# Three elementwise steps put on GpSimd in a four-layer sequence model, and one of two products with ones left out

## The chip, the cores and the metric

The kernel runs on one core of one Trainium2 chip. The metric is the device time of one execution in microseconds (us), the median over several runs. The profile lists the core's engines: PE (TensorE products) and PEld (its weight loads), DVE (VectorE), ACT (ScalarE), POOL (GpSimd) and SP (which issues the DMAs here).

## What is computed

A sequence of 256 tokens of width 1024 passes two blocks of two layers each. The first block has, twice, a mixer (compressed, selected and sliding-window attention, a gated linear attention and a pooling branch) and a feed-forward part. The second block puts 16 meta tokens in front (272 rows) and has a layer of a gated linear recurrence (RG-LRU) beside attention over a sliding window with sinks, a layer of the Mamba-2 kind, and a feed-forward part behind each. Cut to what the change touches:

```python
# first block, sliding-window and selected attention
p = masked_softmax(s, m)                      # e / sum(e)
return jnp.einsum('bhgqk,bgkd->bhgqd', p, vb) # times a sigmoid gate per branch

# second block, first layer
y_a = gelu(gate) * rg_lru(xr, ...)            # the recurrence's gating
p_band = p_band / denom; p_meta = p_meta / denom

# second block, second layer (8 groups of 256 channels)
yg = yg * lax.rsqrt(jnp.mean(yg * yg, axis=-1, keepdims=True) + EPS)
```

## The kernel before

Activations lie with channels on the 128 partitions and tokens along the free dimension, so a tile is 128 x 256 or 128 x 272 (128 x 258 where the second-last layer needs only its last columns). Weights stream in as f32 chunks of up to 1 MB; each is split into a rounded part (`wh`, ScalarE, L257) and a rest (`wl`, VectorE, L258), and each weight tile of 128 x 128 is multiplied in three passes (`mm3`, L272 to L274). These passes are most of TensorE's 11685 instructions. The order of instructions on every engine is fixed when the program is built, by a scheduler that goes by the program's order and its own costs; `issue_after` puts a piece of work behind a given product, so that attention steps are dealt out between the projections' products. Every engine then works through its own list in order and waits where an operand or a buffer is not ready.

The places that the change touches:

- **`nsa.scores` (L815 to L841)**, first block, called for six (block of 128 tokens, head) pairs in each of its two layers. TensorE writes the scores of two key groups (L825), VectorE adds the mask and takes the maximum (L831), ScalarE takes the exponential and its sum (L833), VectorE the reciprocal and the branch gate (L835, L836), and then VectorE multiplies four pieces of `P` and `Pg` (128 x 128 or 128 x 256) by one number per row (L840). `transposes` (L777 is the shared transposing product) turns `P` and `Pg` for the product with the values.
- **`lru` (L1410 to L1420)**, second block's first layer, 8 tiles `k` of 128 x 272. VectorE takes two products (L1415, L1417), a scan along the tokens (L1419) and the gating `gt = l1 * gt` (L1420). `gt` is split much later (L282, L283) for the output projection.
- **`softmax` (L1467 to L1483)**, in the same layer: `attend` runs for two blocks of tokens and two halves of heads (tile `aP`, 8 pieces of 128 x 272 or 128 x 144) and `attend_meta` once (`aPq`, 2 pieces of 128 x 16). VectorE adds the bias and takes the row maximum while it empties the score banks (L1486), forms the exponent's offset (L1471 to L1473), ScalarE takes the exponentials (L1477), VectorE adds up and inverts (L1479, L1480) and multiplies the pieces (L1483). TensorE then transposes them (L1518 for the meta keys, L1528 for the others).
- **`ssd` (L1751 to L1833)**, second block's second layer, 8 groups `g`. ScalarE squares two tiles `sq` of 128 x 258 (L1828); TensorE adds them up over the partitions by two products with a matrix of ones that add up in one bank (L1832); ScalarE copies the sum out (L1833).

Of the kernel before, what the change touches and what calls it, by code (L numbers as in the profile page):

```python
# [10 lines left out]
OP = mybir.AluOpType  # L11
# [127 lines left out]
def view(ap, off, dims):  # L139

    return bass.AP(tensor=ap.tensor, offset=ap.offset + off, ap=[list(ap.ap[0])] + [list(d) for d in dims])
# [37 lines left out]
class Kern:  # L179
# [594 lines left out]
    def nsa(self, l, qT, kT, vsb, vc, sg, mh, ml):  # L774
        nc, p1, w1 = self.nc, self.p1, self.w1
        mm, V, A = nc.tensor.matmul, nc.vector, nc.scalar
# [38 lines left out]
        def scores(t, h):  # L815

            W = 128 * (t + 1)
            sp = [self.bank(x) for x in ("dd", "cb", "da", "ad", "ad", "ad")[3 * t + h]]
            P = (w1.tile([128, 512], F32, name="P", tag="P", bufs=3),
                 p1.tile([128, 512], F32, name="Pg", tag=f"tb{(h + t) % 2}"))  # L820
            m = w1.tile([128, 2, 2], F32, name="m2", tag="m2", bufs=4)
            sm = w1.tile([128, 2, 2], F32, name="s2", tag="s2", bufs=4)
            for b in range(2):

                self.pair(lambda g: mm(sp[g][:, b * W:b * W + W], lhsT=qT[gp[g], h, qs[t]], rhs=kT[gp[g], 1 + b, 0:W],  # L825
                                       start=True, stop=True))
            for b in range(2):
                for g in range(2):
                    c = slice(b * W, b * W + W)

                    V.tensor_tensor_reduce(P[g][:, c], sp[g][:, c], nm[:, 128 * t:128 * t + W], scale=-0.125,  # L831
                                           scalar=3.0e38, op0=OP.add, op1=OP.min, accum_out=m[:, b, g:g + 1])
                    A.activation(P[g][:, c], P[g][:, c], AF.Exp, scale=-1.0, bias=m[:, b, g:g + 1],  # L833
                                 accum_out=sm[:, b, g:g + 1])
            V.reciprocal(sm, sm)  # L835
            V.tensor_tensor(sm, sm, view(sg, t * 18 + 6 + 2 * h, [[6, 2], [1, 2]]), op=OP.mult)  # L836
            for g in range(2):
                for b in range(2):
                    c = slice(b * W, b * W + W)
                    V.tensor_scalar(P[g][:, c], P[g][:, c], sm[:, b, g:g + 1], None, op0=OP.mult)  # L840
            state[t, h] = P  # L841

        def transposes(t, h):
# [28 lines left out]
        def end(t):  # L872
            self.split(mh[:, 5:8, qs[t]], ml[:, 5:8, qs[t]], o[t][:, 0:384].rearrange("p (h q) -> p h q", h=3))
        compressed(0)
        scores(0, 0)
        yield
        scores(0, 1)
        yield
        compressed_T(0)
# [3 lines left out]
        for i, (t, h) in enumerate(heads):  # L883
            transposes(t, h)
            yield
            if h == 0:
                begin(t)
            outputs(t, h)
            if h == 2:
                end(t)  # L890
            if i + 2 < 6:
                scores(*heads[i + 2])
            if i == 1:
                compressed_T(1)
            yield
# [203 lines left out]
class Kern2(Kern):  # L1099
# [263 lines left out]
    def griffin(self, h, rs, feed):  # L1363
        nc, a, p1, w1 = self.nc, self.a, self.p1, self.w1
        V, A, mm = nc.vector, nc.scalar, nc.tensor.matmul
# [5 lines left out]
        gt = p1.tile([128, 8, T2], F32, name="lgt")  # L1371
# [38 lines left out]
        def lru(k):  # L1410

            l1 = w1.tile([128, T2], F32, name="ll1", tag="ll1", bufs=3)
            A.activation(l1, tt[:, k], AF.Ln, scale=-1.0, bias=1.0)
            A.activation(tt[:, k], tt[:, k], AF.Ln, scale=-0.5, bias=self.eps(1e-37))
            V.tensor_tensor(l1, tt[:, k], l1, op=OP.subtract)  # L1415
            A.activation(l1, l1, AF.Exp, scale=0.5)
            V.tensor_tensor(l1, l1, xc[:, k], op=OP.mult)  # L1417
            A.activation(tr[:, k], tr[:, k], AF.Exp, scale=sp[:, k:k + 1], bias=sp[:, k:k + 1])
            V.tensor_tensor_scan(l1, tr[:, k], l1, 0.0, op0=OP.mult, op1=OP.add)  # L1419
            V.tensor_tensor(gt[:, k], l1, gt[:, k], op=OP.mult)  # L1420

        def ev_x(m, o):
            self.conv4(xc[:, m], self.scaled(o, rs), "l", m)
# [35 lines left out]
        for c in range(3):  # L1459
            qkv(c, bank=self.gbank)  # L1460
            with self.tc.issue_after(self.last.ins):
                for k in range(3 * c, min(3 * c + 3, 8)):
                    lru(k)
# [3 lines left out]
        def softmax(P, m, hs, nsk, scales):  # L1467


            n = P.shape[1]  # L1470
            V.tensor_tensor(m[:, 0, :, :n], m[:, 0, :, :n], hs, op=OP.mult)  # L1471
            V.tensor_tensor(m[:, 0, :, :n], m[:, 0, :, :n], nsk, op=OP.min)
            V.tensor_tensor(m[:, 1, :, :n], m[:, 0, :, :n], nsk, op=OP.subtract)  # L1473
            A.activation(m[:, 1, :, :n], m[:, 1, :, :n], AF.Exp)
            for i in range(n):
                for kv in range(2):
                    A.activation(P[:, i, kv], P[:, i, kv], AF.Exp, scale=scales(kv, i), bias=m[:, 0, kv, i:i + 1],  # L1477
                                 accum_out=m[:, 2, kv, i:i + 1])
            V.tensor_tensor(m[:, 2, :, :n], m[:, 2, :, :n], m[:, 1, :, :n], op=OP.add)  # L1479
            V.reciprocal(m[:, 2, :, :n], m[:, 2, :, :n])  # L1480
            for i in range(n):
                for kv in range(2):
                    V.tensor_scalar(P[:, i, kv], P[:, i, kv], m[:, 2, kv, i:i + 1], None, op0=OP.mult)  # L1483

        def scores(P, sc, b, m):
            V.tensor_tensor_reduce(P, sc, b, scale=-0.125, scalar=3.0e38, op0=OP.add, op1=OP.min, accum_out=m)  # L1486
# [3 lines left out]
        def attend(blk, hb, par):  # L1490
# [11 lines left out]
            for i0 in range(0, 4, per):  # L1502
# [7 lines left out]
                if i0 == 1:  # L1510
                    yield
            hv = lambda t, o: view(t, o + hb * 4, [[8, 2], [1, 4]])
            softmax(P, m, hv(slope, 0), hv(ns, 0), lambda kv, i: -SLOPES[kv * 8 + hb * 4 + i])
            yield
            PM = w1.tile([32, 512], F32, name="aPM", tag="aPM")
# [37 lines left out]
        def attend_meta():  # L1553

            V.tensor_copy(qM, qT[:, :, 0:16])
            P = w1.tile([128, 1, 2, 16], F32, name="aPq", tag="aPq")
            m = w1.tile([128, 3, 2, 4], F32, name="am", tag="am")
            sc = [self.bank(t) for t in ("a", "d")]
            for kv in range(2):
                mm(sc[kv][:, 0:16], lhsT=qM[KP[kv]].rearrange("p a b -> p (a b)"), rhs=kT[KP[kv], (256, 0)[kv]:(272, 16)[kv]],  # L1560
                   start=True, stop=True)
            for kv in range(2):
                scores(P[:, 0, kv], sc[kv][:, 0:16], bias[:, 416:432], m[:, 0, kv, 0:1])
            hv = lambda t, o: view(t, o, [[1, 2], [1, 1]])
            softmax(P, m, hv(slope, 16), hv(ns, 16), lambda kv, i: slope[:, 26 + kv:27 + kv])
            yield
            pt = self.bank("b")
            nc.tensor.transpose(pt[0:32, 0:128], P.rearrange("p a b c -> p (a b c)"), self.ident)
            PM = w1.tile([32, 512], F32, name="aPM", tag="aPM")
            A.activation(PM[:, 0:128], pt[0:32, 0:128], AF.Copy)  # L1570
            yield
            o = self.bank("c")
            mm(o[:, 0:128], lhsT=vM, rhs=PM[:, 0:128], start=True, stop=True)
            ov = o[:, 0:128].rearrange("p (a t) -> p a t", a=8)
            self.split(yb[0][:, :, 0:16], yb[1][:, :, 0:16], ov)
            yield
# [22 lines left out]
    def mamba(self, h, rs, feed):  # L1599
        nc, a, p1, w1 = self.nc, self.a, self.p1, self.w1  # L1600
        V, A, mm, tr = nc.vector, nc.scalar, nc.tensor.matmul, nc.tensor.transpose
        X = self.X
        Z = [p1.tile([128, 8, T2], F32R, name=f"sz{i}") for i in range(2)]
        lo = 14
# [28 lines left out]
        b = self.bank("b")  # L1633
# [117 lines left out]
        def ssd(g, B, C, x, zz, yb, W, W0, e2):  # L1751
# [50 lines left out]
            for q in range(2):  # L1802
                for c in range(2):
                    mm(yo[:, q * 256 + c * 128:q * 256 + c * 128 + 128],
                       lhsT=pv[:, c, 2 * q:2 * q + 2].rearrange("p h d -> p (h d)"),
                       rhs=C[:, 16 + 128 * c:144 + 128 * c], start=True, stop=True)
            yd = self.bank("a")
            for q in range(2):
                for c in range(2):
                    for e in range(2):  # L1810
                        mm(yd[e * 64:e * 64 + 64, q * 256 + c * 128:q * 256 + c * 128 + 128],
                           lhsT=xd[:, c, 2 * q + e], rhs=W[:, c, 2 * q + e], start=True, stop=True)
            y0 = self.bank("c")
            for q in range(2):
                for e in range(2):
                    mm(y0[e * 64:e * 64 + 64, q * 16:q * 16 + 16], lhsT=xd0[:, 2 * q + e], rhs=W0[:, 2 * q + e],
                       start=True, stop=True)
# [4 lines left out]
            for j in range(2):  # L1822
                V.scalar_tensor_tensor(yb[:, j, lo:], x[:, j, lo:], self.v("dsk", 2 * g + j), yb[:, j, lo:],
                                       op0=OP.mult, op1=OP.add)
            V.tensor_tensor(yb[:, :, lo:], yb[:, :, lo:], zz[:, :, lo:], op=OP.mult)
            sq = [self.nrm.tile([128, T2], F32, name="sq", tag="sq", bufs=3) for _ in range(2)]
            for j in range(2):
                A.activation(sq[j][:, lo:], yb[:, j, lo:], AF.Square)  # L1828
            yield
            ss = self.bank("b")[:, lo:T2]  # L1830
            for j in range(2):
                mm(ss, lhsT=self.ones, rhs=sq[j][:, lo:], start=j == 0, stop=j == 1)  # L1832
            A.activation(ssqs[g // 4][:, g % 4, lo:], ss, AF.Copy)  # L1833

        def rstd(half):
# [68 lines left out]
```

## Time and profile before

| | us |
|---|---|
| median of 3 runs (1483.31 to 1486.48) | 1483.72 |
| the profiled execution | 1484.41 |
| its span in the trace | 1482.4 |
| TensorE busy (share of the span) | 1452.2 (98%) |
| VectorE busy | 1120.8 (76%) |
| ScalarE busy | 979.1 (66%) |
| GpSimd busy, 11 instructions | 3.2 |

A span is the time from the first to the last instruction of the trace; the execution's own time has 2.0 us around it. A row of the timeline gives start, duration, engine, line, operation, output and inputs, shape and count. Durations of neighbouring rows overlap, since an instruction starts while the one before it drains; what an instruction takes of its engine's time is the distance to the next start. What stands in brackets behind a row is idle time in front of it and what ended it.

### The profile page before, as it was taken

The numbers are of one execution on the slowest core, as the hardware profiler recorded it, in microseconds if no ns is written. First come the engines' busy times: TensorE is split into PE (matmuls) and PEld (weight loads), VectorE is DVE, ScalarE is ACT, GpSimd is POOL, SyncE is SP. The second block draws the span as 40 slices with busy tenths as digits, with TensorE's granted clock in tenths as the row PEclk, the third lists the DMA queues.
The fourth block names the chain that finished last, engine by engine and source line by source line (L and its number), as shares of the span: only waits on it lengthen the run. The fifth ranks groups of instructions, "written<-read, shape, count | busy, mean of one in ns | idle before, by whom it ended". The sixth has DMA issues, their size and how long they took to land.

```text
span 1482.4 us, 29165 instructions
## 1 busy us (share of the span) xinstructions
PE 1452.2 (98%) x11685; PEld 1390.7 (94%) x11685; DVE 1120.8 (76%) x2242; ACT 979.1 (66%) x1895; POOL 3.2 (0%) x11
## 2 busy tenths in 40 slices
PE   8999999999999999999999999999999999999998
PEld 8889999998889999999879999999889999999998
DVE  5878965568779765577965999745998887799853
ACT  5577754448568654376864787745898885598752
POOL 0000000000000000000000000000000000000000
PEclk9999999999999999999999999999999999999999
DMA  7533555554234655554224345453655543445551
GB/s 248 181 105 138 198 178 188 182 188 147 75 129 143 228 196 175 184 183 141 103 100 146 126 171 200 157 175 117 203 189 177 177 150 126 159 145 204 200 173 48
DMA packets 43559, 239.05 MB, mean 161 GB/s; under 512 B 6272, under 2 KB 11296, under 8 KB 20384
## 3 DMA queue, kind: packets, MB, share of 16 engines
q1 hardware_dynamic: 42912, 235.39, 46.0%
q8 instruction: 91, 1.49, 0.4%
q10 hardware_dynamic: 512, 1.80, 0.4%
q14 instruction: 44, 0.36, 0.1%
HBM read 236.09 MB, written 1.08 MB: 160 GB/s over the span
## 4 chain that ended last, share of the span: by engine, by line
PE 87%; ACT 5%; DVE 5%; DMA 1%; issue 1%; SPq 0%; DVEq 0%; ACTq 0%
PE mm L272 11%; PE mm L274 10%; PE mm L273 10%; PE a L272 7%; PE a L273 7%; PE a L274 7%; PE b L272 3%; PE b L274 3%; PE c L273 3%; PE b L273 3%; PE c L274 3%; PE c L272 3%; DVE wl L258 1%; PE d L272 1%; PE d L274 1%; PE d L273 1%
## 5 line engine op out<-in xcount | busy, mean ns | idle before, releaser
L258 DVE TENSOR_TENSOR wl<-raw,wh 128x1024 fp32r<-128x1024 f32 (+3 forms) x448 | 518.4, 1162 | 218.3 <-ACT wh L257 216.8
L257 ACT ACTIVATE wh<-raw 128x1024 fp32r<-128x1024 f32 (+3 forms) x448 | 449.8, 1009 | 309.7 <-PE mm L273 127.7
L272 PE MATMUL mm<-xh,wh 128*128 128x256 f32 (+2 forms) x656 | 191.8, 293 | 2.9 <-ACT wh L257 2.6
L274 PE MATMUL mm<-xh,wl 128*128 128x256 f32 (+2 forms) x656 | 187.6, 286 | 1.9 <-DVE wl L258 1.9
L273 PE MATMUL mm<-xl,wh 128*128 128x256 f32 (+2 forms) x656 | 186.9, 285 | 0.0
L272 PEld LDWEIGHTS mm<-xh,wh 128*128 128x128 f32 x656 | 123.9, 189 | 8.2 <-ACT wh L257 3.2
L274 PEld LDWEIGHTS mm<-xh,wl 128*128 128x128 f32 x656 | 124.1, 189 | 2.8 <-DVE wl L258 2.6
L273 PEld LDWEIGHTS mm<-xl,wh 128*128 128x128 f32 x656 | 123.9, 189 | 1.0 <-issue 0.3
L272 PE MATMUL a<-xh,wh 128*128 128x256 f32 (+2 forms) x416 | 119.4, 289 | 1.7 <-ACT xh L1186 1.5
L273 PE MATMUL a<-xl,wh 128*128 128x256 f32 (+2 forms) x416 | 119.4, 287 | 0.0
L274 PE MATMUL a<-xh,wl 128*128 128x256 f32 (+2 forms) x416 | 118.5, 286 | 0.0
L274 PE MATMUL mm<-hh,wl 128*128 128x256 f32 (+1 forms) x292 | 82.7, 283 | 0.0
L273 PE MATMUL mm<-hl,wh 128*128 128x256 f32 (+1 forms) x292 | 82.6, 283 | 0.0
L272 PE MATMUL mm<-hh,wh 128*128 128x256 f32 (+1 forms) x292 | 82.6, 283 | 0.0
L272 PEld LDWEIGHTS a<-xh,wh 128*128 128x128 f32 x416 | 78.9, 190 | 3.0 <-ACT xh L1186 2.6
L273 PEld LDWEIGHTS a<-xl,wh 128*128 128x128 f32 x416 | 79.0, 190 | 0.6 <-DVE xl L1187 0.2
L274 PE MATMUL a<-hh,wl 128*128 128x256 f32 (+1 forms) x280 | 79.3, 283 | 0.0
L272 PE MATMUL a<-hh,wh 128*128 128x256 f32 (+1 forms) x280 | 79.1, 282 | 0.0
L273 PE MATMUL a<-hl,wh 128*128 128x256 f32 (+1 forms) x280 | 79.0, 282 | 0.0
L274 PEld LDWEIGHTS a<-xh,wl 128*128 128x128 f32 x416 | 78.9, 190 | 0.1
L272 PE MATMUL mm<-sz,wh 128*128 128x258 f32 (+1 forms) x208 | 61.9, 298 | 0.5 <-ACT yn L1215 0.3
L272 PE MATMUL b<-xh,wh 128*128 128x256 f32 (+2 forms) x208 | 59.8, 287 | 0.1
(617 smaller groups left out, 4403.7 us busy)
## 6 DMA issues: line engine op xcount, KB each, us to landing
raw<-fupb SPq DMA_DIRECT2D x40, 1024.0 KB, 4.8
raw<-wdn SPq DMA_DIRECT2D x32, 1024.0 KB, 4.8
raw<-wupb SPq DMA_DIRECT2D x28, 1024.0 KB, 4.8
raw<-bin SPq DMA_DIRECT2D x22, 1024.0 KB, 5.0
raw<-fdna SPq DMA_DIRECT2D x16, 1024.0 KB, 4.8
raw<-ain SPq DMA_DIRECT2D x11, 1024.0 KB, 4.8
raw<-win SPq DMA_DIRECT2D x8, 768.0 KB, 5.8
raw<-fdnb SPq DMA_DIRECT2D x8, 768.0 KB, 4.3
```

The lines of the kernel that those rows point to most:

```text
L257: nc.scalar.activation(h, raw[:, s:s + piece], AF.Copy)
L258: nc.vector.tensor_tensor(l, raw[:, s:s + piece], h, op=OP.subtract)
L272: mm(out, lhsT=lh, rhs=rh, start=first, stop=False, **kw)
L273: mm(out, lhsT=lh, rhs=rl, start=False, stop=False, **kw)
L274: self.pe = mm(out, lhsT=ll, rhs=rh, start=False, stop=last, **kw)
```

## The change

GpSimd takes four elementwise steps: the multiplication by inverse sums in both softmaxes (L840: 48 instructions, L1483: 34), the gating of the recurrence (L1420: 8), and a new sum of the two squared tiles (8). With the sum, one product with ones is left of two in each of the 8 groups.

```diff
@@ nsa.scores
-                    V.tensor_scalar(P[g][:, c], P[g][:, c], sm[:, b, g:g + 1], None, op0=OP.mult)
+                    nc.gpsimd.tensor_scalar(P[g][:, c], P[g][:, c], sm[:, b, g:g + 1], None, op0=OP.mult)
@@ lru
-            V.tensor_tensor(gt[:, k], l1, gt[:, k], op=OP.mult)
+            nc.gpsimd.tensor_tensor(gt[:, k], l1, gt[:, k], op=OP.mult)
@@ softmax
-                    V.tensor_scalar(P[:, i, kv], P[:, i, kv], m[:, 2, kv, i:i + 1], None, op0=OP.mult)
+                    nc.gpsimd.tensor_scalar(P[:, i, kv], P[:, i, kv], m[:, 2, kv, i:i + 1], None, op0=OP.mult)
@@ ssd
+            nc.gpsimd.tensor_tensor(sq[0][:, lo:], sq[0][:, lo:], sq[1][:, lo:], op=OP.add)
             yield
             ss = self.bank("b")[:, lo:T2]
-            for j in range(2):
-                mm(ss, lhsT=self.ones, rhs=sq[j][:, lo:], start=j == 0, stop=j == 1)
+            mm(ss, lhsT=self.ones, rhs=sq[0][:, lo:], start=True, stop=True)
```

The scheduler also orders the lists anew around these places. GpSimd's own list gets the 98 instructions in the program's order, and in front of the first L840 an instruction without operands or waits that readies GpSimd's code. SP's list of DMAs stays as it was.

On TensorE, in group 0 of `ssd` (`sz` is the layer's input, `sq` a squared tile), the difference reads:

```order
@@ -7604,5 +7604,4 @@
 L273 MATMUL d<-sz_12441,wh 128x272
 L274 MATMUL d<-sz_12440,wl 128x272
-L1832 MATMUL b<-sq,ones 128x258 x2
 L272 MATMUL d<-sz_12440,wh 128x272
 L273 MATMUL d<-sz_12441,wh 128x272
@@ -7610,4 +7609,5 @@
 L272 MATMUL d<-sz_12440,wh 128x272
 L273 MATMUL d<-sz_12441,wh 128x272
+L1832 MATMUL b<-sq,ones 128x258
 L274 MATMUL d<-sz_12440,wl 128x272
 L272 MATMUL d<-sz_12440,wh 128x272
```

The one product that is left stands five passes of the projection further back. It is so in groups 0 and 7 alone; in the six others it stands where the two stood.

On VectorE, at the end of the eight `lru` tiles and the first score reductions (`ll` is `l1`, `am` and `aP` belong to the first softmax of the second block):

```order
 L258 TENSOR_TENSOR wl<-raw,wh 128x1024
-L1420 TENSOR_TENSOR lgt<-ll_8760,lgt 128x272
 L1417 TENSOR_TENSOR ll_8769<-ll_8769,lxc 128x272
+L258 TENSOR_TENSOR wl<-raw,wh 128x1024
+L1419 SCALAR_TENSOR_TENSOR ll_8769<-ltr,ll_8769 128x272
 L1486 ISA aP,am<-a,abias 128x272
 L1486 ISA am 128x1
-L1419 SCALAR_TENSOR_TENSOR ll_8769<-ltr,ll_8769 128x272
 L1486 ISA aP,am<-d,abias 128x272
 L1486 ISA am 128x1
-L1420 TENSOR_TENSOR lgt<-ll_8769,lgt 128x272
```

The last scan now stands ahead of the first score reduction instead of behind it, and no gating is left between. Three splits L258 stand ahead of that reduction in both orders. Further on, a split more stands ahead of the first L1471 than before, and the split that stood right ahead of the first L1483 is gone from there.

On TensorE, at the transposes of that first softmax, before:

```order
L1528 MATMUL b<-ident,aP 128x128 x2
L1518 MATMUL c<-ident,aP 32x128
L1528 MATMUL b<-ident,aP 128x128 x2
L1518 MATMUL c<-ident,aP 32x128
L272 MATMUL mm<-xh,wh 128x272
L1518 MATMUL c<-ident,aP 32x128
L1528 MATMUL b<-ident,aP 128x128 x4
L1518 MATMUL c<-ident,aP 32x128
```

and now:

```order
L1528 MATMUL b<-ident,aP 128x128 x2
L1518 MATMUL c<-ident,aP 32x128
L1528 MATMUL b<-ident,aP 128x128 x2
L273 MATMUL mm<-xl,wh 128x272
L1518 MATMUL c<-ident,aP 32x128
L274 MATMUL mm<-xh,wl 128x272
L272 MATMUL mm<-xh,wh 128x272
L273 MATMUL mm<-xl,wh 128x272
L1518 MATMUL c<-ident,aP 32x128
L274 MATMUL mm<-xh,wl 128x272
L272 MATMUL mm<-xh,wh 128x272
L1518 MATMUL c<-ident,aP 32x128
```

The four heads' L1518 now have one, three and two passes of the projection between them. From the first score product (L1505) of this softmax to its first transpose there were 84 passes and are now 70; its second batch of score products, which needs banks that L1486 has emptied, stood behind 30 of them and now stands behind 18. At the second such softmax (the other half of the heads) TensorE's order is unchanged.

## Rows read from the trace of the kernel before

**Rows 1.** The page's part 1: busy time, share of the span, instructions of each engine.
```profile
PE 1452.2 (98%) x11685; PEld 1390.7 (94%) x11685; DVE 1120.8 (76%) x2242; ACT 979.1 (66%) x1895; POOL 3.2 (0%) x11
```

**Rows 2.** TensorE's waits: line, released by, us in total, times, longest.
```profile
PE d L1505 <- DVE am L1486: 1.9, 1, 1.9
PE c L1542 <- ACT aPM L1519: 0.5, 1, 0.5
```

**Rows 3.** Timeline of GpSimd, its first fills: start, duration, engine, line, operation, shape.
```profile
0.73 0.74 POOL L411 MEMSET azero<- 128x768 f32 x1 [0.29 <-POOLq L1896]
1.40 1.06 POOL L431 MEMSET S<- 64x1152 f32 x1
2.40 0.12 POOL L433 MEMSET kcb<- 128x32 f32 x1
```

**Rows 4.** Timeline of TensorE, the products with ones of groups 0, 1 and 7.
```profile
1087.75 1.03 PE L1832 MATMUL b<-sq,ones 128*128 128x258 f32 x4
...
1109.03 1.03 PE L1832 MATMUL b<-sq,ones 128*128 128x258 f32 x4
1109.90 0.27 PE L1770 MATMUL a<-ident,sx 128*128 128x128 f32 x1
...
1244.18 0.49 PE L1832 MATMUL b<-sq,ones 128*128 128x258 f32 x1
```

**Rows 5.** Timeline of ScalarE, the squares of groups 0 and 7.
```profile
1086.91 0.71 ACT L1828 ACTIVATE sq<-yn 128x258 f32<-128x258 f32 x2
...
1243.72 0.71 ACT L1828 ACTIVATE sq<-syb 128x258 f32<-128x258 f32 x2
```

**Rows 6.** Timeline of VectorE beside these squares.
```profile
1087.03 1.22 DVE L1763 TENSOR_TENSOR sW<-sW,scm 128x1024 f32<-128x1024 f32 x1
...
1243.85 1.22 DVE L258 TENSOR_TENSOR wl<-raw,wh 128x1024 fp32r<-128x1024 f32 x1 [1.25 <-ACT wh L257]
```

**Rows 7.** Timeline of VectorE, the recurrence and the second block's first softmax.
```profile
716.68 0.72 DVE L1419 TENSOR_TENSOR_SCAN ll<-ltr,ll 128x272 f32<-128x272 f32 x1
717.43 0.44 DVE L1420 TENSOR_TENSOR lgt<-ll,lgt 128x272 f32<-128x272 f32 x1
717.79 1.22 DVE L258 TENSOR_TENSOR wl<-raw,wh 128x1024 fp32r<-128x1024 f32 x1
...
727.38 0.43 DVE L1486 CUSTOM_DVE_ANT_0 aP<-a,abias 128x272 f32<-128x272 f32 x1
...
731.42 0.50 DVE L1455 SCALAR_TENSOR_TENSOR aqT<-mm,aslope,rs 128x272 f32<-128x272 f32 x1
731.84 0.16 DVE L1471 TENSOR_TENSOR am<-am,aslope 128x8 f32<-128x8 f32 x1
...
737.39 1.17 DVE L258 TENSOR_TENSOR wl<-raw,wh 128x1024 fp32r<-128x1024 f32 x1
738.48 2.25 DVE L1483 TENSOR_SCALAR aP<-aP,am 128x272 f32<-128x272 f32 x8
```

**Rows 8.** Timeline of TensorE in the same stretch.
```profile
728.86 0.49 PE L1505 MATMUL d<-akT,aqT 64*128 64x272 f32 x1 [1.91 <-DVE am L1486]
...
738.89 0.29 PE L274 MATMUL mm<-xh,wl 128*128 128x272 f32 x1
739.02 0.38 PE L1528 MATMUL b<-ident,aP 128*128 128x128 f32 x2
```

**Rows 9.** Timelines of VectorE and TensorE, the other half of the heads.
```profile
760.86 2.26 DVE L1483 TENSOR_SCALAR aP<-aP,am 128x272 f32<-128x272 f32 x8
...
763.78 0.60 PE L1518 MATMUL c<-ident,aP 128*32 128x128 f32 x4
```

**Rows 10.** Timelines of VectorE and TensorE, the first block's sixth softmax.
```profile
118.54 0.16 DVE L836 TENSOR_TENSOR s<-s,sg 128x4 f32<-128x4 f32 x1
...
120.12 0.95 DVE L258 TENSOR_TENSOR wl<-raw,wh 128x768 fp32r<-128x768 f32 x1
...
121.34 0.27 PE L777 MATMUL d<-ident,Pg 128*128 128x128 f32 x1
```

## The prediction, made before the changed kernel ran

> **What bounds the kernel now.** I read the busy times first: TensorE works 1452.2 of 1482.4 us, VectorE 1120.8, ScalarE 979.1, and GpSimd 3.2 [rows 1]. So only two things can move the time by much: work taken off TensorE, and waits put on it. The next view is TensorE's waits, to see which of them the change touches: one of 1.9 us for the score reductions, and one of 0.5 us at the first meta-key product [rows 2]. VectorE's time is not the bound, so the 90 instructions taken off it gain only where TensorE waits for VectorE; the 98 that GpSimd gets cost wherever TensorE then waits for GpSimd. Then I read the timelines at the four places to find, for each moved instruction, when its inputs are there and when TensorE asks for its result.
>
> **GpSimd's prices.** Before, GpSimd only fills tiles. A fill of 768 columns takes 0.67 us to the next start and one of 1152 columns 1.00 [rows 3], so a pass over columns costs 0.86 ns each and nearly nothing besides: 0.23 us for 272. A multiplication by one number per row reads and writes: 0.23 if both overlap, 0.47 if not. A product of two tensors has three passes: 0.23 to 0.70. VectorE's own 0.28 (eight in 2.25) and 0.36 [rows 7] lie between. Nothing shows the passes overlapping, so I take them apart, and with a little for the start: 0.5 and 0.75 us, 0.47 for 256 columns. Ends for the range: 0.25, and a third more.
>
> The Trainium skill, "GPSIMD Engine Reference", section 3.1, gives 4497 ns for adding two tensors of 2048 columns; in proportion that is an estimate of 0.6 us for 272, and the sum below would be about +2.7 by it instead of +4.1.
>
> **Do the engines disturb each other?** Most of what VectorE does beside these instructions combines two tensors in SBUF (its splits, products and scans); 272 columns of two tensors take it 0.36 us, of one tensor 0.28 [rows 7]. So a second operand has a price of its own, and GpSimd's operands may have to be fetched in the same way. The trace cannot show it, since fills read nothing. The ends: VectorE loses nothing to a GpSimd instruction, or all of its length. I take the whole: VectorE is back to back in the stretch that matters, so nothing there would hide a loss. It is my choice, not a reading, and the other end is a rival.
>
> The Trainium skill, "SBUF — State Buffer", section "Who interferes with whom", speaks against this change in the same sense: a VectorE instruction with two SBUF inputs and a GpSimd instruction that reads SBUF exclude each other, and the later one waits for the whole of the earlier. No row here shows it. By that rule the sum is +4.1; by the rows' other end it is -1.8.
>
> **Products with ones.** The four TensorE instructions of two products take 1109.90 - 1109.03 = 0.87 us [rows 4], one product 0.435. Eight groups lose 8 x 0.435 = **-3.5 us**, TensorE's own time. Against it: the sum must now come in between. In group 0 the squares end at 1086.91 + 0.71 = 1087.62 [rows 5]. The product stood at 1087.75 [rows 4] and stands five passes of 0.13 (739.02 - 738.89) [rows 8] later, at 1088.40. Room 0.78, need 0.75 and a hand-over of 0.1. But VectorE holds a product of two tensors until 1088.25 [rows 6]; behind it GpSimd ends at 1089.0: TensorE waits 0.6. In group 7 the squares end at 1244.43 [rows 5], the product stands at 1244.18 + 0.65 = 1244.83 [rows 4], and VectorE splits weights until 1245.07 [rows 6]: GpSimd ends at 1245.8, a wait of 1.0. The other six have at least group 0's room; I give them 0.3 together. Part: -3.5 + 1.9 = **-1.6**.
>
> **Gating.** Seven gatings leave VectorE ahead of the first score reduction at 727.38 and a scan of 0.75 (716.68 to 717.43) comes ahead of it [rows 7]: 727.38 - 7 x 0.36 + 0.75 = 725.6. If each gating keeps VectorE off for 0.75, less about 0.42 each (731.42 to 731.84) [rows 7] for the three query evacuations, which read a bank and one tensor and run beside one: + 7 x 0.75 - 1.26, so 729.6. TensorE was ready for its second batch of scores at 728.86 - 1.91 = 726.95 [rows 8]; with 12 passes fewer ahead, it is at 725.4. It needs two reductions of 0.4 done: 730.4. It waits 5.0 instead of 1.9: **+3.1**. Behind the waiting product are all of TensorE's next ones; nothing passes it.
>
> **First softmax of the second block.** From the first reduction to L1471 a scan and a gating go (0.75 + 0.36) and a split (1.1) comes, so L1471 and the inverse sums come 2.2 later like the reduction, at 737.39 + 2.2 = 739.6 (the split at 737.39 that VectorE ran ahead of its first multiplication at 738.48 [rows 7] is out of the way). GpSimd's first two pieces are done at 740.6 to 740.7. TensorE asks for them at 739.02 [rows 8] + 3.1 - 14 x 0.13 = 740.3: a wait of 0.3. Then each head takes GpSimd 1.0, while TensorE has between them the passes shown in the order and transposes of 0.11 (0.22 for two, 0.60 for four with their tail): 0.7, 0.5, 0.4. Waits: 0.3 + 0.5 + 0.6. The 0.5 at the meta-key product [rows 2] falls away, since passes now stand there. Part: 0.3 + 1.4 - 0.5 = **+1.2**.
>
> **The other softmaxes.** For the other half of the heads VectorE multiplies from 760.86 to 763.1 and TensorE's fourth L1518 stands at 763.78 + 0.33 = 764.1 [rows 9]. GpSimd ends at 760.9 + 8 x 0.5 = 764.9: **+0.8**. The pieces of 144 columns and the meta queries have microseconds of room by the order: nothing. In the first block the tightest is the sixth softmax: gate ready by 118.7, four pieces of 0.47 end at 120.7, TensorE asks for the second pair's result at 121.34 [rows 10]. Room 0.6; if the split at 120.12 comes in between with its 0.87, 0.25 is missing. I take 0.3 a layer with the fourth softmax, which is nearly as tight: **+0.6** for two layers. GpSimd's code being readied costs nothing: it stands behind fills that end by 4 us and is wanted near 90. VectorE's freed 22 us elsewhere are worth nothing, because TensorE does not wait for them.
>
> **Sum.** -1.6 + 3.1 + 1.2 + 0.8 + 0.6 = **+4.1 us** on the profiled 1484.41: 1488.5. The median of the runs lies 0.7 below the profiled one, so I forecast 1483.72 + 4.1 = **1487.8**. A difference under 0.2% (3.0 us) cannot be told from none here.
>
> **Rivals.**
> 1. *The engines do not disturb each other.* For it: no row shows them doing so. Then group 0 and 7 wait 0.55 together, TensorE's second batch comes at 726.4 and waits 1.0 (-0.9), the first softmax costs +1.2 as before, the other half +0.8, the first block nothing: -3.5 + 0.55 - 0.9 + 1.2 + 0.8 = -1.8, so **1481.9**, no measurable change.
> 2. *GpSimd is as fast as its fills* (0.25 for both kinds), from where the kernel is not slower but faster: TensorE waits nowhere new, the 0.5 and 0.9 fall away: **1479.0**. For it: the fills. Against: reading is work too. It decides below about 0.35 us for 272 columns, without disturbance.
> 3. *GpSimd is a third dearer* (0.65 and 1.0): gating 3.1 + 7 x 0.25 = +4.9, first softmax 1.2 + 8 x 0.15 = +2.4, other half 0.8 + 8 x 0.15 = +2.0, first block some 0.45 more a layer, +1.5, groups 1.9 + 2 x 0.25 = +2.4 against -3.5: +9.7, **1493.4**; at twice the price some 1507.
> 4. *The product's removal gives nothing*, because each group waits for its sum as long as the product took: only if GpSimd needs over 1.2 us there. With no loss elsewhere: **1484**.
>
> **Chances.** Forecast 0.42 (its own range 1485.5 to 1491), rival 1 0.25, rival 2 0.12, rival 3 0.15, rival 4 0.06. The range of 8 in 10 runs from rival 1 with some luck to rival 3: 1480 to 1494; it leaves out most of rival 2 and the far end of rival 3. Faster by over 0.2%: rival 2 and a little of rival 1, 0.15. Slower: rival 3 and most of the forecast, 0.49. Same: 0.36.
>
> **What would show it.** Right: eight products fewer of 0.43; GpSimd rows of 128 x 272 that start 0.5 (one tensor) and 0.75 us (two) apart; VectorE's products of two tensors longer or later wherever a GpSimd row runs; TensorE's largest wait at L1505, about 5 us, and new waits of 0.3 to 1 us at L1518 and L1832. Wrong: VectorE's rows as long as before beside GpSimd's, and the L1505 wait at 1 us (rival 1); L1518 released without a wait (rival 2); waits over 1 us in the first block's transposes (rival 3).

## The result, and the profile after

Five runs of the changed kernel have a median of 1505.34 us (1501.47 to 1507.67), beside 1483.88 for the kernel before. The ratio, estimated from all runs and not from the two medians, is 1.0137, 95% interval 1.0119 to 1.0154: 20.3 us slower (17.7 to 22.9). Forecast was +4.1, with a range up to 1494. The profiled execution took 1501.47 with a span of 1499.7; it is the fastest of the five and has the highest mean granted clock (0.991, the others 0.939 to 0.990), so the trace shows somewhat less than the whole loss.

The page's part 1, and from its part 2 the granted clock in 40 slices:

```profile
PE 1455.7 (97%) x11669; PEld 1389.9 (93%) x11669; DVE 1108.5 (74%) x2152; ACT 980.9 (65%) x1895; POOL 87.8 (6%) x109
PEclk9999999999999999999889999999999999999999
```

Against [rows 1]: TensorE has 16 instructions less (a product here is two rows) but is busy 3.5 us longer, VectorE only 12 us shorter, though 90 instructions have left it, and GpSimd busy 88 instead of 3. In two of the 40 slices the granted clock is below 0.9, which it was nowhere before.

TensorE's longest waits (what waits, for what; total, times, longest):

```profile
PE c L1518 <- POOL aP L1483: 8.0, 7, 2.1
PE d L1505 <- DVE am L1486: 3.1, 1, 3.1
...
PE b L1832 <- POOL sq L1829: 1.9, 3, 0.9
PE d L777 <- POOL Pg L840: 1.7, 4, 0.5
...
PE b L1528 <- POOL aP L1483: 0.6, 1, 0.6
```

[Rows 2] had the second of these, at 1.9 us, and none of the others. To see where the time comes in, I compared the starts of ScalarE's and VectorE's instructions that stand in both traces (after minus before, us):

| stretch (time before) | late at its start | late at its end | added |
|---|---|---|---|
| loads ahead of the first block, to 60 | 0 | -2.4 | -2.4 |
| first block's two softmaxes (86 to 130, 387 to 444) | -2.4, -1.7 | -1.8, -1.1 | +1.2 |
| second block's first layer, 704 to 807 | -1.1 | 17.2 | **+18.3** |
| Mamba groups, 1086 to 1278 | 17.0 | 17.3 | +0.3 |
| to the end | 17.3 | 17.3 | 0 |

The first line differs from profile to profile (-3.0 to +1.0 in those below) and is nothing of the change. The rest is one layer. Its first softmax on TensorE (the last column of a waiting row is idle time and what ended it):

```profile
739.22 0.29 PE L274 MATMUL mm<-xh,wl 128*128 128x272 f32 x1
739.35 0.29 PE L272 MATMUL mm<-xh,wh 128*128 128x272 f32 x1
740.22 0.44 PE L1528 MATMUL b<-ident,aP 128*128 128x128 f32 x2 [0.58 <-POOL aP L1483]
741.16 0.29 PE L1518 MATMUL c<-ident,aP 128*32 128x128 f32 x1 [0.51 <-POOL aP L1483]
...
743.04 0.40 PE L1518 MATMUL c<-ident,aP 128*32 128x128 f32 x1 [1.25 <-POOL aP L1483]
...
743.46 0.43 PE L272 MATMUL mm<-xh,wh 128*128 128x272 f32 x1
743.69 0.43 PE L273 MATMUL mm<-xl,wh 128*128 128x272 f32 x1
744.92 0.39 PE L1518 MATMUL c<-ident,aP 128*32 128x128 f32 x1 [0.81 <-POOL aP L1483]
...
746.81 0.40 PE L1518 MATMUL c<-ident,aP 128*32 128x128 f32 x1 [1.03 <-POOL aP L1483]
```

Two things happen here. Every head waits for GpSimd, 4.2 us in all. And the passes, 0.13 apart at 739.22, are 0.23 apart at 743.46. The view by windows tells why (span, then busy time and instructions of PE, PEld, DVE, ACT, POOL, the granted clock, the DMA share, GB/s):

```profile
738.00:741.00 3.00, 2.07 (x15) 1.61 (x14) 1.02 (x5) 3.00 (x17) 1.81 (x2) 1.00 0.94 333
741.00:744.00 3.00, 1.59 (x8) 1.18 (x8) 0.58 (x2) 0.77 (x3) 3.00 (x5) 0.79 0.04 16
744.00:747.00 3.00, 1.16 (x6) 0.73 (x5) 0.00 (x0) 0.00 (x0) 3.00 (x4) 0.50 0.00 0
747.00:750.00 3.00, 3.00 (x11) 2.06 (x10) 0.47 (x1) 1.84 (x5) 3.00 (x6) 0.50 0.02 5
...
756.00:759.00 3.00, 3.00 (x29) 2.50 (x28) 2.72 (x5) 3.00 (x4) 0.00 (x0) 0.94 0.00 0
```

The granted clock falls from 1.00 (2.4 GHz) to 0.50 (1.2 GHz) amid the waits and stays there until 756.4, though TensorE is busy without a break from 747 on. It is at 0.50 in three stretches: 729.1 to 732.5, behind the 3.1 us at L1505; 742.7 to 756.4; and 776.9 to 783.7, amid the same kind of waits for the other half of the heads. Between 710 and 810 TensorE idles 12.9 us, against 3.3 before: +9.6. Its busy time in each half microsecond, times what the clock lacks of 1.00, adds up to 9.8 us. Together 19.4, a little above the 18.3 of the table: a pass at half clock takes 0.23 instead of 0.13, which is less than twice as long. So the loss in this trace is **half waits, half clock**.

GpSimd's prices, by groups (busy in total, mean ns of one), and the starts of three neighbours:

```profile
L1483 POOL TENSOR_SCALAR aP<-aP,am 128x272 f32<-128x272 f32 x16 | 15.6, 995 | 29.2 <-ACT aP L1530 18.9 <-ACT aP L1477 10.3
...
L1829 POOL TENSOR_TENSOR sq<-sq 128x258 f32<-128x258 f32 x8 | 9.1, 1137 | 455.4 <-ACT sq L1828 455.4
...
L1420 POOL TENSOR_TENSOR lgt<-ll,lgt 128x272 f32<-128x272 f32 x8 | 7.4, 923 | 71.2 <-ACT ll L1416 62.8 <-DVE ll L1419 6.2 <-ACT ltr L1418 1.1
```
```profile
739.19 0.97 POOL L1483 TENSOR_SCALAR aP<-aP,am 128x272 f32<-128x272 f32 x1 [10.29 <-ACT aP L1477]
...
740.14 0.96 POOL L1483 TENSOR_SCALAR aP<-aP,am 128x272 f32<-128x272 f32 x1
...
741.08 0.96 POOL L1483 TENSOR_SCALAR aP<-aP,am 128x272 f32<-128x272 f32 x1
```

The multiplication by one number takes 0.94 us from start to start where I had put 0.5. A product of two tensors lasts 0.76 in the shortest gating, close to the 0.75 that I had put, and up to 1.60 where something is in its way.

What is in its way shows on VectorE. Its two products of the recurrence, by groups:

```profile
L1417 DVE TENSOR_TENSOR ll<-ll,lxc 128x272 f32<-128x272 f32 x8 | 5.3, 657 | 0.9 <-ACT ll L1416 0.9
L1415 DVE TENSOR_TENSOR ll<-ltt,ll 128x272 f32<-128x272 f32 x8 | 4.4, 548 | 0.1
```

Before, both had a mean of 0.43 us and none over 0.44. Now six of the sixteen last 0.78 to 1.00, each beside a gating on GpSimd. The longest one, the gating beside it, and what TensorE waits for behind them:

```profile
722.44 0.72 PE L1505 MATMUL a<-akT,aqT 64*128 64x272 f32 x2 [0.60 <-DVE aqT L1455]
...
724.33 1.60 POOL L1420 TENSOR_TENSOR lgt<-ll,lgt 128x272 f32<-128x272 f32 x1 [1.43 <-DVE ll L1419]
...
725.22 1.00 DVE L1417 TENSOR_TENSOR ll<-ll,lxc 128x272 f32<-128x272 f32 x1
...
727.92 0.41 DVE L1486 CUSTOM_DVE_ANT_0 aP<-a,abias 128x272 f32<-128x272 f32 x1
...
728.75 0.55 PE L1505 MATMUL d<-akT,aqT 64*128 64x272 f32 x1 [3.13 <-DVE am L1486]
```

The 0.60 us for a query tile (`aqT`) that VectorE fills late is new; the trace before has no wait there.

### The profile page after: what moved, and what is told of

The parts are those of the page before. It is cut to its first block, busy times and chain, and to the rows that moved or that the text cites. A ratio compares the mean times of both kernels' runs of the same rounds, so it can differ in the third digit from the quotient of the medians.

```text
span 1499.7 us, 29225 instructions
## 1 busy us (share of the span) xinstructions
PE 1455.7 (97%) x11669; PEld 1389.9 (93%) x11669; DVE 1108.5 (74%) x2152; ACT 980.9 (65%) x1895; POOL 87.8 (6%) x109
## 4 chain that ended last, share of the span: by engine, by line
PE 50%; issue 14%; DVE 3%; ACT 2%; POOL 2%; POOLq 0%; DVEq 0%; ACTq 0%
PE mm L272 6%; PE mm L274 6%; PE mm L273 6%; PE a L272 5%; PE a L273 5%; PE a L274 5%; PE c L272 3%; PE c L273 3%; PE c L274 3%; PE b L274 2%; PE b L273 2%; PE b L272 2%; POOL aP L1483 1%; ACT aP L1477 1%; DVE wl L258 1%
## 5 line engine op out<-in xcount | busy, mean ns | idle before, releaser
L258 DVE TENSOR_TENSOR wl<-raw,wh 128x1024 fp32r<-128x1024 f32 (+3 forms) x448 | 520.2, 1167 | 229.8 <-ACT wh L257 228.8
L274 PE MATMUL mm<-sz,wl 128*128 128x258 f32 (+1 forms) x208 | 59.4, 286 | 0.6 <-DVE wl L258 0.6
```

Of the source, the lines that this page charges most:

```text
L258: nc.vector.tensor_tensor(l, raw[:, s:s + piece], h, op=OP.subtract)
L274: self.pe = mm(out, lhsT=ll, rhs=rh, start=False, stop=last, **kw)
```

## The experiments

Ratios are to runs of the kernel before on the same chip, in the same session, and again not those of the medians; the differences are the ratio's, times 1485.

**The four parts, each alone.**

```diff
@@ e1_sum: only this
-                mm(ss, lhsT=self.ones, rhs=sq[j][:, lo:], start=j == 0, stop=j == 1)
+            nc.gpsimd.tensor_tensor(sq[0][:, lo:], sq[0][:, lo:], sq[1][:, lo:], op=OP.add)
+            mm(ss, lhsT=self.ones, rhs=sq[0][:, lo:], start=True, stop=True)
@@ e2_gate: only this
+            nc.gpsimd.tensor_tensor(gt[:, k], l1, gt[:, k], op=OP.mult)
@@ e3_soft: only this
+                    nc.gpsimd.tensor_scalar(P[:, i, kv], P[:, i, kv], m[:, 2, kv, i:i + 1], None, op0=OP.mult)
@@ e4_first: only this
+                    nc.gpsimd.tensor_scalar(P[g][:, c], P[g][:, c], sm[:, b, g:g + 1], None, op0=OP.mult)
```

> Only the sum of the squares on GpSimd and one product with ones. Theory A (the sum in my prediction holds here): eight products of 0.43 us go, three waits of 1.9 us come, 1.6 us faster than before. Rival B (the wait for the sum costs as much as the product): no change, within 0.5 us. Rival C (GpSimd's sums delay VectorE's work for the groups and so the chain): 1 us slower or more. The trace tells B from C by the waits at the product with ones and at the groups' other products.

> Only the recurrence's gating on GpSimd. Theory A (the wait at the second batch of score products grows from 1.9 to 3.1 us and the granted clock then falls to half for some 4 us, a loss of 1.8 us of TensorE's work): 3 us slower. Rival B (the clock falls only where the softmax waits as well, so not here): 1.2 us slower, clock 1.00 through this stretch. Rival C (most of the loss of the changed kernel comes from the two engines holding each other up in this stretch): 8 us slower or more.

> Only the second block's softmax multiplications on GpSimd. Theory A (a multiplication by one number of 128 x 272 takes GpSimd 1.0 us, so TensorE waits 8 us at the transposes of both halves, and the granted clock falls to half for about 15 and 8 us behind these waits): 14 to 16 us slower. Rival B (the waits alone cost, the clock falls only because the gating's wait comes ahead): 8 us slower, clock 1.00. Rival C (gating and softmax each cost about half of the loss): 7 to 9 us slower with the clock falling for less than 5 us.

> Only the first block's softmax multiplications on GpSimd. Theory A (four waits of 0.4 to 0.5 us at the transposes of two layers, less what they hide): 1 to 1.5 us slower, clock 1.00. Rival B (GpSimd's instructions hold up VectorE's in both layers and the delay goes on into the layers behind): over 3 us slower.

| kernel | median | ratio (95% interval) | difference |
|---|---|---|---|
| e1_sum | 1485.93 | 0.9997 (0.9988 to 1.0006) | -0.4 |
| e2_gate | 1486.57 | 1.0004 (0.9995 to 1.0013) | +0.6 |
| e3_soft | 1501.32 | 1.0098 (1.0085 to 1.0112) | **+14.6** |
| e4_first | 1487.18 | 1.0004 (0.9995 to 1.0013) | +0.6 |

*e3_soft*: theory A. In its trace TensorE waits at the transposes as in the whole change, and the clock is at half from 740.9 to 754.5 and from 778.5 to 785.3, so the gating is not needed for that:

```profile
PE c L1518 <- POOL aP L1483: 7.7, 7, 2.1
...
PE d L1505 <- DVE am L1486: 1.9, 1, 1.9
...
PE b L1528 <- POOL aP L1483: 1.3, 1, 1.3
```

*e1_sum*: the 1.6 us of theory A are not there. By the starts in both traces the groups begin 1.85 late and end 2.13 late: +0.3, the same as in the whole change. Groups 1 to 4 and 6 gain 0.3 to 0.4 each; group 0 loses 0.3, group 5 0.5 and group 7 1.3 (its wait, and 0.7 more at the normalised tiles behind it). Group 5, in the trace of the whole change:

```profile
1219.55 1.08 DVE L283 TENSOR_TENSOR xl<-yn,xh 128x258 fp32r<-128x258 f32 x3
...
1220.06 1.57 POOL L1829 TENSOR_TENSOR sq<-sq 128x258 f32<-128x258 f32 x1 [24.78 <-ACT sq L1828]
1220.57 0.47 DVE L1842 SCALAR_TENSOR_TENSOR yn<-yn,vec,sssq 128x258 f32<-128x258 f32 x1
...
1221.68 0.70 PE L1832 MATMUL b<-sq,ones 128*128 128x258 f32 x2 [0.70 <-POOL sq L1829]
```

The sum's row lasts 1.57 behind and beside VectorE's instructions on two tensors; the shortest, in groups 2 and 4, last 0.74.

*e2_gate*: its time, +0.6 (-0.7 to +1.9), allows B's 1.2 and not A's 3, but its trace shows A's mechanism and not B's. The wait at L1505 is 3.1 us as in the whole change, the clock is at half from 726.8, amid this wait, to 733.6, and the trace is 2.3 us later behind this stretch than ahead of it. Other kernels with L1505's old wait lose a part of that too in some of their profiles (last section), which may be why the times show less; that is not shown. C is out. *e4_first*: four waits, 1.7 us, as theory A says; +1.2 in its trace, and by its time no more than that.

**The change without the second block's softmax**, to see whether the parts add up:

```diff
@@ e13_rest: the change, but
-                    nc.gpsimd.tensor_scalar(P[:, i, kv], P[:, i, kv], m[:, 2, kv, i:i + 1], None, op0=OP.mult)
+                    V.tensor_scalar(P[:, i, kv], P[:, i, kv], m[:, 2, kv, i:i + 1], None, op0=OP.mult)
```

> The change without the second block's softmax: that one stays on VectorE, the other three parts are made. Theory A (the parts add up, and the softmax is the loss): 0 to 4 us slower than before, as the three runs of one part each add up to 0.8 by their times and 3.8 by their profiles. Rival B (the parts make each other worse, above all the gating ahead of the softmax): 6 us slower or more.

Measured 1488.09, ratio 1.0022 (1.0013 to 1.0031), +3.3 us: A. One line of the diff, 34 instructions, carries the rest. In the times the parts do not quite add up: 14.6 + 0.6 + 0.6 - 0.4 = 15.4 for the four alone, and 14.6 + 3.3 = 17.9 for e3_soft and e13_rest, beside 20.3 (17.7 to 22.9) for the whole. In the traces they add up to a little more than the whole: 17.9 + 2.3 + 1.2 + 0.3 = 21.7 for the stretches of the four, beside 18.3 + 1.2 + 0.3 = 19.8. What the times leave over is open.

**Price or clock?** Three kernels put only L1483 on GpSimd, in whole or in part, and change one thing each against e3_soft.

```diff
@@ e6_tt: the inverse sum repeated along the columns
+                    nc.gpsimd.tensor_tensor(P[:, i, kv], P[:, i, kv], m[:, 2, kv, i:i + 1].to_broadcast([128, P.shape[3]]), op=OP.mult)
@@ e7_alt: dealt out
+                    (nc.gpsimd if kv else V).tensor_scalar(P[:, i, kv], P[:, i, kv], m[:, 2, kv, i:i + 1], None, op0=OP.mult)
@@ e9_fill: e3_soft, and behind each L1518 of the 272-column softmaxes
+                if blk:
+                    mm(pm[64:128, 0:512], lhsT=self.ident[:, 64:128], rhs=view(P, 2 * i * W, [[1, 512]]), start=True, stop=True)
```

> The second block's softmax multiplications alone on GpSimd, but each as a product of two tensors whose second one is the inverse sum repeated along the columns. Theory A (the form sets GpSimd's time: 0.77 us for 272 columns, as the gating took, instead of 1.0 for a multiplication by one number): pieces of 0.77 us, TensorE's waits at the transposes fall from 9 to 5 or 6 us, and the kernel is 9 to 12 us slower than before, 3 to 6 faster than with the multiplication by one number. Rival B (a product of two tensors reads more and is no faster): 14 to 16 us slower as before, or more.

> The second block's softmax multiplications alone, dealt out: the first of a head's two pieces on VectorE, the second on GpSimd, so that a head takes GpSimd 1.0 us, which is what my prediction gave it. Theory A (the loss grows faster than GpSimd's time, because the granted clock falls only behind the long and close waits): waits at the transposes of 1 to 3 us in total, clock at full speed behind them or at half for less than 5 us, 1 to 4 us slower than before. Rival B (the loss is in proportion to GpSimd's time): half of 14.6, some 7 us slower.

> The second block's softmax multiplications alone on GpSimd, and behind each of the eight transposes that wait for them a product of 512 columns by the identity, whose result nobody reads: TensorE has work in the waits. It reads the piece just multiplied, so it cannot come earlier. Theory A (half of the loss is the granted clock, which falls because TensorE stands idle again and again): the clock stays near full speed and the kernel is 8 to 11 us slower than before, 4 to 7 faster than without the added products, although TensorE does 7 us more. Rival B (the clock falls for another reason, the power of the other engines or the mix of products): the clock falls as before and the added products cost up to 7 us more, 15 to 22 us slower than before.

| kernel | median | ratio (95% interval) | difference | more idle, 710 to 810 | lost at half clock | later, 704 to 807 |
|---|---|---|---|---|---|---|
| e3_soft | 1501.32 | 1.0098 (1.0085 to 1.0112) | +14.6 | 9.0 | 10.9 | 17.9 |
| e6_tt | 1494.16 | 1.0056 (1.0044 to 1.0068) | +8.3 | 4.6 | 6.4 | 10.0 |
| e7_alt | 1492.65 | 1.0042 (1.0028 to 1.0055) | +6.2 | 1.6 | 5.1 | 6.4 |
| e9_fill | 1498.05 | 1.0083 (1.0071 to 1.0095) | +12.3 | 2.5 | 1.7 | 12.9 |

The last three columns are from one profile of each, worked out as above: what TensorE idles more than before, its busy time times what the clock lacks of 1.00, and what the stretch adds.

*e6_tt*: the form matters. The pieces of 272 columns start 0.60 us apart; their mean of 0.75 comes from two that were held up, to 1.44 and 1.62:

```profile
L1483 POOL TENSOR_TENSOR aP<-aP,am 128x272 f32<-128x272 f32 x16 | 11.4, 749 | 107.3 <-DVE am L1480 86.2 <-ACT aP L1530 21.1
L1483 POOL TENSOR_TENSOR aP<-aP,am 128x144 f32<-128x144 f32 x16 | 6.4, 437 | 6.1 <-ACT aP L1530 6.1
```

TensorE's waits at the transposes fall to 4.6 us, and the kernel gains 6.3 us on e3_soft, a little more than theory A had. *e7_alt* is the most telling. A head takes GpSimd about 1.0 us, as my prediction had it, and TensorE's waits for it come to 1.7 us:

```profile
PE c L1518 <- POOL aP L1483: 1.7, 3, 0.7
```

My first-softmax and other-half terms were 2.0 together. But the time is 6.2 (4.2 to 8.2), and 5.1 are lost at half clock: some 1.7 behind the old wait at L1505 (731.9 to 735.3; more on that below) and the rest behind waits of 0.36, 0.59 and 0.71 us for GpSimd and 0.32 for ScalarE between 741.6 and 745.0, after which the clock stays at half from 745.5 to 752.4. So theory A failed on the size of the median: the loss is nearly in proportion to GpSimd's time, as B says, though not for B's reason. The runs differ with the clock: this profile is of the slowest of six (1494.88, mean clock 0.990), while two of them, at 0.996, took 1488.17 and 1489.41, which is what theory A had. *e9_fill* tests the clock. The added products read the piece just multiplied and so run in the waits. Theory A's fall from e3_soft is smaller than it had (2.3 us, not 4 to 7), but B would have had it rise. In the other half, where GpSimd's eight pieces take 8.0 us in both, e3_soft (first fence) and e9_fill (second):

```profile
774.00:777.00 3.00, 0.28 (x1) 0.09 (x1) 0.68 (x4) 0.00 (x0) 3.00 (x4) 1.00 0.55 172
777.00:780.00 3.00, 2.12 (x9) 1.73 (x10) 0.00 (x0) 1.34 (x2) 0.83 (x1) 0.74 0.43 180
780.00:783.00 3.00, 3.00 (x12) 1.30 (x12) 1.23 (x1) 3.00 (x16) 0.00 (x0) 0.50 0.00 0
```
```profile
774.00:777.00 3.00, 1.98 (x5) 0.57 (x6) 0.00 (x0) 0.00 (x0) 2.25 (x3) 1.00 0.80 328
777.00:780.00 3.00, 3.00 (x14) 1.57 (x13) 0.07 (x1) 1.75 (x4) 0.00 (x0) 1.00 0.01 3
```

With work in the waits the clock does not fall here at all, and in the first half for 3.4 us instead of 13.7. The kernel is faster although TensorE does some 8 us more (from the start of one added product, at 740.49, to the next product, at 741.51, are 1.02, and there are eight). That idling makes the clock fall is shown by this, and not by the one profile alone: the five runs of e9_fill have mean clocks of 0.995 to 0.998, the four of e3_soft 0.988 to 0.991. The added products eat most of what the clock gives back.

**What keeps VectorE waiting: reads or any work of GpSimd?** Three fills (1.09 us together, at least as long as most gatings), in the gating's place, with the gating itself on VectorE:

```diff
@@ e10_memset: the kernel before, and behind L1420
+            for _ in range(3):
+                nc.gpsimd.memset(l1, 0.0)
```

> The kernel before, and behind each of the eight gatings, which stay on VectorE, three fills of 128 x 272 on GpSimd over the tile just used up, about 0.75 us: GpSimd writes to SBUF as long as a gating took it, and reads nothing. Theory A (a GpSimd instruction that reads SBUF keeps VectorE's instructions on two tensors in SBUF waiting, one that only writes does not): the products at L1415 and L1417 beside the fills last 0.43 us as without them. Rival B (any GpSimd work in SBUF does): several of them last 0.6 to 1.0 us, as beside the gating on GpSimd. Time: within 2 us of before by A.

One run, 1482.26 us. The same two groups:

```profile
L1415 DVE TENSOR_TENSOR ll<-ltt,ll 128x272 f32<-128x272 f32 x8 | 3.4, 431 | 0.0
L1417 DVE TENSOR_TENSOR ll<-ll,lxc 128x272 f32<-128x272 f32 x8 | 3.4, 434 | 0.9 <-ACT ll L1416 0.9
```

Eight of the sixteen run beside a fill, and none lasts over 0.44: theory A, in one profile. What collides with VectorE's instructions on two tensors is not GpSimd's writing; what the gating does besides is to read.

**Versions that might beat both.** The sum on VectorE; the gating later on VectorE; and both.

```diff
@@ e5_sumv: as e1_sum, but
+            V.tensor_tensor(sq[0][:, lo:], sq[0][:, lo:], sq[1][:, lo:], op=OP.add)
@@ e11_late: scan into tt[:, k], no gating in lru, and ahead of the splits of gt
+            V.tensor_tensor(gt[:, k], tt[:, k], gt[:, k], op=OP.mult)
@@ e12_both: e5_sumv and e11_late
```

> Only the sum of the squares, on VectorE instead of GpSimd, and one product with ones. Theory A (eight products of 0.43 us are worth 3.5 us, and on GpSimd it was the waits in groups 0, 5 and 7, behind sums held up to 1.5 us, that took the gain; VectorE's sum takes 0.36): waits of at most 1 us in all, 2 to 3 us faster than before. Rival B (the sum on VectorE comes as late, since it queues behind VectorE's other work, up to 2 us in a group): no change, within 1 us, with waits at the product with ones of 2 us or more.

> The gating stays on VectorE but is moved behind, in the program, to the splits that need it (the scan keeps its result in another tile); the scheduler puts three of the eight behind the first score reductions. Theory A (VectorE's work ahead of the first reductions sets the wait of 1.9 us at the second batch of score products): the wait falls by about 0.7 to 1.1 us and the clock does not fall behind it, 1 to 3 us faster than before. Rival B (the wait is set by the splits and the products that remain): no change, within 1 us.

> Gating moved behind on VectorE, and the sum of the squares on VectorE with one product with ones; GpSimd takes nothing. Theory A (the two gains lie in different layers and add up): 3 to 5 us faster than before. Rival B (only the sum's gain is there): 1 to 2.5 us faster.

| kernel | median | ratio (95% interval) | difference |
|---|---|---|---|
| e5_sumv | 1483.77 | 0.9988 (0.9979 to 0.9997) | -1.8 |
| e11_late | 1483.55 | 0.9989 (0.9980 to 0.9998) | -1.6 |
| e12_both | 1484.04 | 0.9989 (0.9980 to 0.9998) | -1.6 |

All three are faster than before by about a thousandth, less than the 0.2% of the prediction, with intervals that end just below 1. e5_sumv has no wait at the product with ones; a wait of 1.4 us at the convolution's tile (L1345) is new and takes a part of the 3.5. In e11_late the wait at L1505 is 2.2 us, not less than 1.9: its theory A is not what happened, and where its gain lies is open. The two gains do not add up. The traces say why in part: the sum's stretch, 1086 to 1278, is 1.6 us shorter in e5_sumv and again in e12_both, while the layer of the gating, 704 to 807, comes out 0.1 longer in e11_late and in e12_both. So the sum's gain is the one that can be seen; that e12_both has only this one is its rival B.

## Why the prediction was wrong, step by step

- **GpSimd's prices**: the step that failed first. "0.5 and 0.75 us" came from fills, with passes taken apart. Measured: 0.94 from start to start for 272 columns times one number, and 0.76 for the shortest gating, so the second price held and the first was nearly twice as high. The pass model failed for the first form: 144 columns take 0.62 and 272 take 0.94, which is 2.5 ns a column with 0.26 us besides, where I had two passes of 0.86 ns and next to nothing besides. The order of the two forms was reversed, and of the 34 of the expensive kind the sixteen of 272 columns stood on the path. The Trainium skill, "GPSIMD Engine Reference", section 3.1, gave an estimate of 0.6 us for two tensors, which the 0.60 of e6_tt's product bears out and the gating's 0.76 does not; it has no time for the other form, which the runs show to be dearer.
- **First softmax and other half**, +2.0: mis-sized by that price, waits of 8.6 us instead of 2.5 (0.3 + 1.4 + 0.8; the sum took off 0.5). At the price I had put (e7_alt) the waits came out below that, 1.7.
- **The clock**: missing from the sum. None of its terms had a price for what TensorE's work takes after a wait. The trace of before gave no hint of it: behind its wait of 1.9 us [rows 2] the clock stayed at 1.00 (the last section has the row). It cost up to 9.8 us, half of the loss in the trace.
- **Rival 3** gave 1507 for twice the price, near the 1505 measured. That was luck: it made all of it waits on GpSimd, in all places alike. The price was twice only for one form, and half of the time was the clock.
- **Do the engines disturb each other?** Right in kind. The Trainium skill, "SBUF — State Buffer", section "Who interferes with whom", says that one waits for the whole of the other; L1415 and L1417 (0.43 to as much as 1.00) and GpSimd's own 1.57 and 1.60 agree, and e10_memset shows that fills, which only write, do not do it. The size was nearly right too: VectorE was held up 3.1 us (six products, and a split of 1.68 instead of 1.22) where I had 4.0, and its first score reduction, at 727.92 in a trace that runs 1.1 us ahead here, comes 0.6 earlier than forecast. **Gating**, +3.1, was mis-sized on TensorE's side: the wait at L1505 grew to 3.1 us, not 5.0, mostly because TensorE came to it 1.3 us later than I had it (725.6, or 726.7 in the time of before, not 725.4), 0.6 of that for the new wait for a query tile. The one-part run shows +0.6 (-0.7 to +1.9).
- **Products with ones**, -1.6: no gain (-0.4 by the run, +0.3 in the traces). The 0.43 us for a product hold. Groups 0 and 7 waited nearly as forecast (0.4 and 0.9); group 5, to which I gave no wait of its own, waited 0.7, because VectorE held GpSimd up there.
- **First block**, +0.6: mis-sized by the price again, +1.2 in the trace, clock at 1.00 throughout. The price for 256 columns was 0.90 from start to start, not 0.47. As said, nothing waited for GpSimd's code, and no stretch of the table shows a gain from VectorE's freed time.

## What to carry to other kernels

Work taken off an engine that is not the bound gained nothing here; look at what the new engine's instruction costs in exactly that form, and whether the bounding engine waits for it. Where TensorE is the bound, count a new wait on it twice: once as it stands, once for the work behind it that may run at half clock, above all where several waits come close together. If elementwise work has to go to GpSimd, then where VectorE runs neither instructions on two tensors in SBUF nor multiplications by one number at that time, and a multiplication by one number per row as a product with that number repeated; here even that (e6_tt) was 8.3 us slower than VectorE.

## What was not expected of the hardware

- On GpSimd, 272 columns times one number per row start 0.94 us apart, times a second tensor that is this number repeated (e6_tt) 0.60; for 144 columns 0.62 and 0.38. A product of two whole tensors, the gating, lasts 0.76 at best, while e6_tt's pieces last 0.64; why the two differ is open.
- VectorE's multiplication by one number, 0.27 us apart alone, starts 0.50 apart beside GpSimd's (e7_alt; before, eight took 2.25 [rows 7]):

```profile
740.02 2.05 DVE L1483 TENSOR_SCALAR aP<-aP,am 128x272 f32<-128x272 f32 x4
```

- The same wait of 1.9 us at L1505 has the clock at 1.00 behind it in five profiles of eight with this wait (the kernel before, e4, e5, e6 and e9), and at half for 3.4 us in three (e1, e3, e7). With 2.2 us (e11, e12) and 3.1 us (the whole change, e2, e13) the clock fell in all five. The kernel before and e1_sum, which differ only in a later layer, in the same window:

```profile
729.00:731.00 2.00, 1.97 (x15) 1.33 (x16) 1.91 (x10) 0.00 (x0) 0.00 (x0) 1.00 0.97 410
```
```profile
729.00:731.00 2.00, 2.00 (x13) 1.89 (x14) 1.46 (x9) 0.00 (x0) 0.00 (x0) 0.52 0.48 201
```

  It cost e1_sum 0.8 us there.
- In a later layer, where nothing of L1483 or L1420 lies, TensorE waits in every profile for the rest of a split weight (`wl`, L258). The rows of the kernel before and of e7_alt:

```profile
1065.08 0.39 PE L274 MATMUL mm<-xh,wl 128*128 128x258 f32 x1 [1.44 <-DVE wl L258]
```
```profile
1073.98 0.58 PE L274 MATMUL mm<-xh,wl 128*128 128x258 f32 x1 [2.87 <-DVE wl L258]
```

  This wait is 1.4 us in the kernel before and in the whole change, and the clock stays at 1.00 around it. In ten of the other twelve profiles it is 2.1 to 2.9 us, and the clock is at half for 3.4 to 10.2 us from there. The same stretch thus costs some kernels' profiles a microsecond or more that is not their change. The times of the kernel before spread with the clock too (1483.5 with a mean clock of 0.998, 1489.7 with 0.992); where the clock fell in those runs is not on record.
